# Residual-add LayerNorm on one Trainium2 core: one-pass variance, gamma and beta spread by a matmul, other chunk lists

## The chip, the cores and the metric

The kernel runs on one NeuronCore of one Trainium2 chip. The metric is device time in microseconds (us) of one execution. Most executions of one kernel here agree within about 0.3%. For one execution of each kernel there is a profile; its span (first to last instruction) is about 2 us shorter than the time.

Engines: VectorE (DVE in the profile), ScalarE (ACT), TensorE (PE), GpSimd (POOL), and SyncE (SP). SyncE and ScalarE issue DMAs on hardware queues, GpSimd on a software queue.

## The reference

```python
# x, residual: 16 x 1024 x 512 float32; gamma = ones(512), beta = zeros(512), eps = 1e-5
z = x + residual
mean = np.mean(z, axis=-1, keepdims=True)
var = np.var(z, axis=-1, keepdims=True)
return gamma * (z - mean) / np.sqrt(var + eps) + beta      # float32
```

16,384 rows of 512 numbers: 33.55 MB each for x, the residual and the output, 100.7 MB in all. There is no matmul in the task.

## The kernel before

The rows are cut into 128 blocks of 128 rows. A chunk is r blocks (r = 4 in the body, 1 or 2 at the ends). For each chunk SyncE loads x and the residual (1 MiB each for r = 4); `produce` makes the sum and the statistics; `consume`, one chunk later, scales, multiplies by gamma, adds beta, and stores from GpSimd, whose DMA casts float16 to float32.

```python
BODY_R = 4
HEAD_CHUNKS = [2, 2]
TAIL_CHUNKS = [2, 2, 1, 1, 1, 1]
BUFS = 9                      # buffers of each tile
ACT_APPLY_FRAC = 0.5          # share of a chunk's blocks that ScalarE scales

nc.gpsimd.dma_start(out=g_t[:], in_=gamma.partition_broadcast(P))   # g_t, b_t: 128 x 512 float16
nc.gpsimd.dma_start(out=b_t[:], in_=beta.partition_broadcast(P))

# produce (one chunk)
nc.sync.dma_start(out=xt[:, 0:r_cur, :], in_=x_ap)
nc.sync.dma_start(out=rt[:, 0:r_cur, :], in_=r_ap)
for n in range(r_cur):                               # VectorE: z = x + residual, S = sum of z
    nc.vector.tensor_tensor_reduce(out=xt[:, n, :], in0=xt[:, n, :], in1=rt[:, n, :],
        op0=ALU.add, op1=ALU.add, accum_out=S[:, n:n+1], ...)
nc.scalar.mul(nmean, S, -inv_D)
for n in range(r_cur):                               # ScalarE: Qc = sum of (z - mean)^2
    nc.scalar.activation(out=junk[:], in_=xt[:, n, :], func=AF.Square,
        bias=nmean[:, n:n+1], accum_out=Qc[:, n:n+1])
nc.scalar.activation(out=std, in_=Qc, func=AF.Sqrt, bias=eps_t[:], scale=inv_D)
nc.vector.reciprocal(out=rstd, in_=std)
nc.vector.tensor_mul(nmr, nmean, rstd)

# consume (the chunk before)
n_act = int(round(r_cur * ACT_APPLY_FRAC))           # 2 of 4, 1 of 2, 0 of 1
for n in range(r_cur):
    if n < n_act: nc.scalar.activation(out=ot[:, n, :], in_=xt[:, n, :], func=AF.Identity,
                      bias=nmr[:, n:n+1], scale=rstd[:, n:n+1])
    else:         nc.vector.tensor_scalar(out=ot[:, n, :], in0=xt[:, n, :], scalar1=nmean[:, n:n+1],
                      scalar2=rstd[:, n:n+1], op0=ALU.add, op1=ALU.mult)
nc.vector.tensor_mul(ot, ot, g_b)                    # float16, whole chunk
nc.vector.tensor_add(ot, ot, b_b)
nc.gpsimd.dma_start(out=o_ap, in_=ot[:, 0:r_cur, :])
# ... (cut: allocation, the loop produce(i), consume(i - 1), the launch)
```

The program is a list for each engine whose order a scheduler fixes when the kernel is built. The list is worked off in that order, so an instruction that waits holds back what is behind it (the run with the longer tail list, below, shows VectorE idle for 1.42 us in front of such an instruction).

## Time and profile before

| | before |
|---|---|
| time, median of 5 | 254.42 us (254.24 to 254.47) |
| span of the profiled run | 252.5 us |
| DMA rate in the body | 416 to 430 GB/s |
| VectorE busy / ScalarE busy | 77% / 67% of the span |
| last 4-block load pair used by VectorE from | 223.69 us |
| VectorE's last instruction ends | 247.50 us |

From the page of the kernel before: the GB/s moved in each of 40 equal slices, the chain of waits by line, and two groups of instructions (engine, operation, output <- inputs, count | busy us, mean ns of one | idle before). L107 is line 107 of the kernel as it was run; line numbers differ between the two kernels. POOLq, SPq and DVEq are the engines' queues.

```profile
GB/s 207 360 428 416 424 427 421 423 422 423 421 427 419 426 424 422 423 421 426 423 421 427 422 426 422 418 430 422 423 422 421 426 426 418 422 414 392 249 319 106
...
DMA rt<-in_residual_dram 91%; POOL out_dram L170 1%; DVE ot L157 1%; DVE ot L167 1%; DVE xt L94 1%; DVE ot L168 0%; POOLq L213 0%; SPq L85 0%; DVE nmr L126 0%; DVE rstd L123 0%; DVE S L94 0%; POOLq L170 0%; DVEq L94 0%
...
L107 ACT ACTIVATE junk<-xt,nmean 128x512 f32<-128x512 f32 x128 | 88.4, 691 | 4.0
...
L157 DVE TENSOR_SCALAR ot<-xt,nmean,rstd 128x512 f16<-128x512 f32 x66 | 33.2, 539 | 0.0
```

The reader sees a flat plateau near 423 GB/s between a weak head and a weak tail: the body is bound by DMA. "91%" means that nearly the whole chain which ends last is landing of residual loads. The square takes 691 ns for a 128x512 block.

The next line is from the view of waits (who waited for whom: us in total, times, longest): VectorE, the busiest compute engine, waited 26 times for loads, so in the body it has time to spare.

```profile
DVE xt L94 <- DMA rt<-in_residual_dram: 40.5, 26, 4.7
```

The head in 1 us windows (window, length, busy us of the engines, TensorE clock, DMA share, GB/s), and the two broadcast loads in the view of DMAs (KB, us from issue to landing):

```profile
core 0: us, DVE busy (x) ACT busy (x) POOL busy (x), PEclk, DMA share, GB/s
...
4.00:5.00 1.00, 0.00 (x0) 0.00 (x0) 0.00 (x0) 1.00 0.93 337
5.00:6.00 1.00, 0.47 (x1) 0.00 (x0) 0.00 (x0) 1.00 0.63 135
6.00:7.00 1.00, 0.85 (x4) 0.12 (x1) 0.00 (x0) 1.00 1.07 335
7.00:8.00 1.00, 0.00 (x0) 0.94 (x4) 0.00 (x0) 1.00 0.80 216
```

```profile
g_t<-in_gamma_dram POOLq DMA_DIRECT2D x1, 128.0 KB, 6.6
b_t<-in_beta_dram POOLq DMA_DIRECT2D x1, 128.0 KB, 8.7
```

DMA share is the mean busy share of the 16 DMA engines. There is a hole of 135 GB/s at 5 to 6 us, in which the DMA engines are busy for only 0.63 of the time, and less than full rate until 9 us, while the broadcasts of gamma and beta are under way (until about 8 and 11 us).

The tail on VectorE in the timeline (start, us, instruction, [idle before]):

```profile
223.69 0.69 DVE L94 CUSTOM_DVE_ANT_0 xt<-xt,rt 128x512 f32<-128x512 f32 x1 [1.50 <-DMA rt<-in_residual_dram]
...
224.98 0.16 DVE L126 TENSOR_TENSOR nmr<-nmean,rstd 128x4 f32<-128x4 f32 x1
...
226.28 1.00 DVE L157 TENSOR_SCALAR ot<-xt,nmean,rstd 128x512 f16<-128x512 f32 x2
...
227.80 1.22 DVE L167 TENSOR_TENSOR ot<-ot,g_t 128x2048 f16<-128x2048 f16 x1
...
246.05 0.54 DVE L157 TENSOR_SCALAR ot<-xt,nmean,rstd 128x512 f16<-128x512 f32 x1
246.62 0.42 DVE L167 TENSOR_TENSOR ot<-ot,g_t 128x512 f16<-128x512 f16 x1
247.08 0.42 DVE L168 TENSOR_TENSOR ot<-ot,b_t 128x512 f16<-128x512 f16 x1
```

A sum appears as two instructions, CUSTOM_DVE_ANT_0 and DVE_READ_ACCUMULATOR2_ANT. At 223.69 the last 4-block pair has landed. VectorE then makes sums (L94), between them finishes the statistics of the chunk before (nmr), scales that chunk (L157), and multiplies it by gamma (L167). It is busy nearly without gap for 23.8 us, until 247.50; 5.0 us later the span ends.

### The profile page before, as it was taken

The numbers are of one execution on the slowest core, as the hardware profiler recorded it, in microseconds if no ns is written. First come the engines' busy times: TensorE is split into PE (matmuls) and PEld (weight loads), VectorE is DVE, ScalarE is ACT, GpSimd is POOL, SyncE is SP. The second block draws the span as 40 slices with busy tenths as digits, with TensorE's granted clock in tenths as the row PEclk, the third lists the DMA queues.
The fourth block names the chain that finished last, engine by engine and source line by source line (L and its number), as shares of the span: only waits on it lengthen the run. The fifth ranks groups of instructions, "written<-read, shape, count | busy, mean of one in ns | idle before, by whom it ended". The sixth has DMA issues, their size and how long they took to land.

```text
span 252.5 us, 1223 instructions
## 1 busy us (share of the span) xinstructions
DVE 195.7 (77%) x471; ACT 168.2 (67%) x394; POOL 21.3 (8%) x43
## 2 busy tenths in 40 slices
DVE  1255899999678877788788886789877888779992
ACT  2374888888456785676786664787665688569760
POOL 2000000000000000000000000000000000000221
DMA  6999999999999999999999999999999999999693
GB/s 207 360 428 416 424 427 421 423 422 423 421 427 419 426 424 422 423 421 426 423 421 427 422 426 422 418 430 422 423 422 421 426 426 418 422 414 392 249 319 106
DMA packets 16282, 101.01 MB, mean 400 GB/s; under 512 B 1808, under 2 KB 2064, under 8 KB 5136
## 3 DMA queue, kind: packets, MB, share of 16 engines
q1 hardware_dynamic: 10656, 67.11, 69.4%
q0 software_dynamic: 5616, 33.82, 34.5%
q14 instruction: 10, 0.08, 0.1%
HBM read 67.63 MB, written 33.55 MB: 401 GB/s over the span
## 4 chain that ended last, share of the span: by engine, by line
DMA 91%; issue 3%; DVE 3%; POOL 1%; POOLq 0%; SPq 0%; DVEq 0%
DMA rt<-in_residual_dram 91%; POOL out_dram L170 1%; DVE ot L157 1%; DVE ot L167 1%; DVE xt L94 1%; DVE ot L168 0%; POOLq L213 0%; SPq L85 0%; DVE nmr L126 0%; DVE rstd L123 0%; DVE S L94 0%; POOLq L170 0%; DVEq L94 0%
## 5 line engine op out<-in xcount | busy, mean ns | idle before, releaser
L94 DVE CUSTOM_DVE_ANT_0 xt<-xt,rt 128x512 f32<-128x512 f32 x128 | 84.6, 680 | 40.5 <-DMA rt<-in_residual_dram 40.5
L107 ACT ACTIVATE junk<-xt,nmean 128x512 f32<-128x512 f32 x128 | 88.4, 691 | 4.0
L149 ACT ACTIVATE ot<-xt,nmr,rstd 128x512 f16<-128x512 f32 x62 | 47.3, 806 | 56.4 <-DVE nmr L126 56.4
L167 DVE TENSOR_TENSOR ot<-ot,g_t 128x2048 f16<-128x2048 f16 (+2 forms) x37 | 39.9, 1078 | 3.9 <-ACT ot L149 1.0
L168 DVE TENSOR_TENSOR ot<-ot,b_t 128x2048 f16<-128x2048 f16 (+2 forms) x37 | 39.9, 1078 | 1.1
L170 POOL DMA_DIRECT2D out_dram<-ot x37 | 19.9, 539 | 225.9 <-ACT junk L107 197.8
L157 DVE TENSOR_SCALAR ot<-xt,nmean,rstd 128x512 f16<-128x512 f32 x66 | 33.2, 539 | 0.0
L107 ACT ACTIVATION_READ_ACCUMULATOR junk<-xt,nmean 128x1 f32 x128 | 23.8, 186 | 0.0
L105 ACT ACTIVATE nmean<-S 128x4 f32<-128x4 f32 (+2 forms) x37 | 7.1, 191 | 15.0 <-DVE S L94 15.0
L115 ACT ACTIVATE std<-Qc,eps_t 128x4 f32<-128x4 f32 (+2 forms) x37 | 11.0, 296 | 1.1
L123 DVE RECIPROCAL rstd<-std 128x4 f32<-128x4 f32 (+2 forms) x37 | 6.3, 169 | 5.5 <-ACT std L115 5.3
L94 DVE DVE_READ_ACCUMULATOR2_ANT S<- 128x1 f32 x128 | 10.4, 81 | 0.0
L126 DVE TENSOR_TENSOR nmr<-nmean,rstd 128x4 f32<-128x4 f32 (+2 forms) x37 | 5.8, 156 | 0.1
L105 ACT ACT_TABLE_LOAD x1 | 1.3, 1283 | 0.7 <-PEq L199 0.7
L115 ACT ACT_TABLE_LOAD x1 | 1.3, 1283 | 0.0
L68 POOL DMA_DIRECT2D g_t<-in_gamma_dram x1 | 0.7, 669 | 0.8 <-PEq L213 0.8
L71 DVE MEMSET eps_t<- 128x1 f32 x1 | 0.1, 59 | 0.8 <-PEq L199 0.8
L69 POOL DMA_DIRECT2D b_t<-in_beta_dram x1 | 0.5, 540 | 0.0
L199 POOL MEMSET const-float32-0.0<- 128x1 f32 x1 | 0.1, 98 | 0.2 <-issue 0.2
L199 POOL MEMSET const-bfloat16-1.0<- 128x1 bf16 x1 | 0.1, 101 | 0.0
L199 POOL MEMSET const-uint8-127<- 128x1 uint8 x1 | 0.1, 99 | 0.0
L199 POOL MEMSET const-float32-1.0<- 128x1 f32 x1 | 0.1, 98 | 0.0
## 6 DMA issues: line engine op xcount, KB each, us to landing
xt<-in_x_dram SPq DMA_DIRECT2D x29, 1024.0 KB, 29.6
rt<-in_residual_dram SPq DMA_DIRECT2D x29, 1024.0 KB, 29.7
out_dram<-ot POOLq DMA_DIRECT2D x29, 1024.0 KB, 9.4
xt<-in_x_dram SPq DMA_DIRECT2D x4, 512.0 KB, 16.6
rt<-in_residual_dram SPq DMA_DIRECT2D x4, 512.0 KB, 16.2
out_dram<-ot POOLq DMA_DIRECT2D x4, 512.0 KB, 6.3
xt<-in_x_dram SPq DMA_DIRECT2D x4, 256.0 KB, 11.9
rt<-in_residual_dram SPq DMA_DIRECT2D x4, 256.0 KB, 9.6
```

Of the source, the lines that this page charges most:

```text
L68: nc.gpsimd.dma_start(out=g_t[:], in_=gamma.partition_broadcast(P))
L94: nc.vector.tensor_tensor_reduce(out=xt[:, n, :], in0=xt[:, n, :], in1=rt[:, n, :], scale=1.0, scalar=0.0, op0=ALU.add, op1=ALU.add, accum ...
L105: nc.scalar.mul(nmean[:, 0:r_cur], S[:, 0:r_cur], -inv_D)
L107: nc.scalar.activation(out=junk[:], in_=xt[:, n, :], func=AF.Square, bias=nmean[:, n : n + 1], accum_out=Qc[:, n : n + 1],)
L115: nc.scalar.activation(out=std[:, 0:r_cur], in_=Qc[:, 0:r_cur], func=AF.Sqrt, bias=eps_t[:], scale=inv_D,)
L123: nc.vector.reciprocal(out=rstd[:, 0:r_cur], in_=std[:, 0:r_cur])
L126: nc.vector.tensor_mul(nmr[:, 0:r_cur], nmean[:, 0:r_cur], rstd[:, 0:r_cur])
L149: nc.scalar.activation(out=ot[:, n, :], in_=xt[:, n, :], func=AF.Identity, bias=nmr[:, n : n + 1], scale=rstd[:, n : n + 1],)
L157: nc.vector.tensor_scalar(out=ot[:, n, :], in0=xt[:, n, :], scalar1=nmean[:, n : n + 1], scalar2=rstd[:, n : n + 1], op0=ALU.add, op1=ALU. ...
L167: nc.vector.tensor_mul(ot[:, 0:r_cur, :], ot[:, 0:r_cur, :], g_b)
L168: nc.vector.tensor_add(ot[:, 0:r_cur, :], ot[:, 0:r_cur, :], b_b)
L170: nc.gpsimd.dma_start(out=o_ap, in_=ot[:, 0:r_cur, :])
```

## The change

Four independent things, besides renaming and reformatting: (1) gamma and beta come as two rows of 2 KB from ScalarE's queue, and a matmul with a column of ones spreads each over 128 partitions; (2) the small head chunks go; (3) the tail list has five chunks instead of six; (4) the variance is taken as E[z^2] - mean^2, so that the square needs no mean and can start after the first block's sum.

```diff
-HEAD_CHUNKS = [2, 2]
-TAIL_CHUNKS = [2, 2, 1, 1, 1, 1]
+HEAD_CHUNKS: list[int] = []
+TAIL_CHUNKS: list[int] = [2, 2, 2, 1, 1]
+CENTERED_STATS = False
+PIPE_DEPTH = 1
-    nc.gpsimd.dma_start(out=g_t[:], in_=gamma.partition_broadcast(P))
-    nc.gpsimd.dma_start(out=b_t[:], in_=beta.partition_broadcast(P))
+    ones = consts.tile([1, P], FP32, name="ones")
+    nc.vector.memset(ones[:], 1.0)
+    nc.scalar.dma_start(out=g_row[:], in_=gamma.unsqueeze(0))
+    nc.scalar.dma_start(out=b_row[:], in_=beta.unsqueeze(0))
+    for row, dst in ((g_row, g_t), (b_row, b_t)):
+        ps = psum.tile([P, D], FP32, ...)
+        nc.tensor.matmul(ps[:], lhsT=ones[:], rhs=row[:], start=True, stop=True)
+        nc.vector.tensor_copy(dst[:], ps[:])
...
         for n in range(r_cur):
             nc.vector.tensor_tensor_reduce(... accum_out=S[:, n : n + 1])
+            nc.scalar.activation(out=junk[:], in_=xt[:, n, :], func=AF.Square,
+                                 accum_out=Qc[:, n : n + 1])
         nc.scalar.mul(nmean, S, -inv_D)
-        for n in range(r_cur):
-            nc.scalar.activation(out=junk[:], in_=xt[:, n, :], func=AF.Square,
-                                 bias=nmean[:, n : n + 1], accum_out=Qc[:, n : n + 1])
-        nc.scalar.activation(out=std, in_=Qc, func=AF.Sqrt, bias=eps_t[:], scale=inv_D)
+        nc.scalar.activation(out=msq, in_=S, func=AF.Square, scale=inv_D)
+        nc.vector.scalar_tensor_tensor(out=var, in0=Qc, scalar=inv_D, in1=msq,
+                                       op0=ALU.mult, op1=ALU.subtract)
+        nc.scalar.activation(out=std, in_=var, func=AF.Sqrt, bias=eps_t[:])
```

The changed file keeps the old statistics behind its flag. With the flag and the other three parts set back, its instruction lists equal those of the kernel before on every engine, so nothing else in the diff matters.

More of the change, by code (lines that the diff above doesn't have):

```diff
@@ L19 @@
 ACT_APPLY_FRAC = 0.5
-DUAL_QUEUE_LOADS = False
+CENTERED_STATS = False
+PIPE_DEPTH = 1
 @with_exitstack
@@ L45 @@
     n_blocks = N // P
-    chunks: list[int] = []
     head = [c for c in HEAD_CHUNKS if c <= BODY_R]
@@ L67 @@
     b_t = consts.tile([P, D], o_dt, name="b_t")
-    nc.gpsimd.dma_start(out=g_t[:], in_=gamma.partition_broadcast(P))
-    nc.gpsimd.dma_start(out=b_t[:], in_=beta.partition_broadcast(P))
+    ones = consts.tile([1, P], FP32, name="ones")
+    nc.vector.memset(ones[:], 1.0)
+    g_row = consts.tile([1, D], FP32, name="g_row")
+    b_row = consts.tile([1, D], FP32, name="b_row")
+    nc.scalar.dma_start(out=g_row[:], in_=gamma.unsqueeze(0))
+    nc.scalar.dma_start(out=b_row[:], in_=beta.unsqueeze(0))
+    for row, dst in ((g_row, g_t), (b_row, b_t)):
+        ps = psum.tile([P, D], FP32, name="ps_" + ("g" if dst is g_t else "b"))
+        nc.tensor.matmul(ps[:], lhsT=ones[:], rhs=row[:], start=True, stop=True)
+        nc.vector.tensor_copy(dst[:], ps[:])
     eps_t = consts.tile([P, 1], FP32, name="eps_t")
@@ L74, with produce @@
     state: list[dict | None] = []
-    def produce(st, base_block, r_cur):
+    def produce(base_block, r_cur):
         rows = P * r_cur
@@ L85, in produce @@
         nc.sync.dma_start(out=xt[:, 0:r_cur, :], in_=x_ap)
-        (nc.scalar if DUAL_QUEUE_LOADS else nc.sync).dma_start(
-            out=rt[:, 0:r_cur, :], in_=r_ap
-        )
+        nc.sync.dma_start(out=rt[:, 0:r_cur, :], in_=r_ap)
         S = stats.tile([P, BODY_R], FP32, name="S")
         Qc = stats.tile([P, BODY_R], FP32, name="Qc")
-        for n in range(r_cur):
-            nc.vector.tensor_tensor_reduce(
-                out=xt[:, n, :],
-                in0=xt[:, n, :],
-                in1=rt[:, n, :],
-                scale=1.0,
-                scalar=0.0,
-                op0=ALU.add,
-                op1=ALU.add,
-                accum_out=S[:, n : n + 1],
-            )
@@ L104, in produce @@
-        nmean = stats.tile([P, BODY_R], FP32, name="nmean")
-        nc.scalar.mul(nmean[:, 0:r_cur], S[:, 0:r_cur], -inv_D)
-        for n in range(r_cur):
-            nc.scalar.activation(
-                out=junk[:],
-                in_=xt[:, n, :],
-                func=AF.Square,
-                bias=nmean[:, n : n + 1],
-                accum_out=Qc[:, n : n + 1],
-            )
-        std = stats.tile([P, BODY_R], FP32, name="std")
-        nc.scalar.activation(
-            out=std[:, 0:r_cur],
-            in_=Qc[:, 0:r_cur],
-            func=AF.Sqrt,
-            bias=eps_t[:],
-            scale=inv_D,
-        )
@@ L122, in produce @@
-        rstd = stats.tile([P, BODY_R], FP32, name="rstd")
+        nmean = stats.tile([P, BODY_R], FP32, name="nmean")
+        std = stats.tile([P, BODY_R], FP32, name="std")
+        rstd = stats.tile([P, BODY_R], FP32, name="rstd")
+        nmr = stats.tile([P, BODY_R], FP32, name="nmr")
+        if CENTERED_STATS:
+            for n in range(r_cur):
+                nc.vector.tensor_tensor_reduce(
+                    out=xt[:, n, :], in0=xt[:, n, :], in1=rt[:, n, :],
+                    scale=1.0, scalar=0.0, op0=ALU.add, op1=ALU.add,
+                    accum_out=S[:, n : n + 1],
+                )
+            nc.scalar.mul(nmean[:, 0:r_cur], S[:, 0:r_cur], -inv_D)
+            for n in range(r_cur):
+                nc.scalar.activation(
+                    out=junk[:], in_=xt[:, n, :], func=AF.Square,
+                    bias=nmean[:, n : n + 1], accum_out=Qc[:, n : n + 1],
+                )
+            nc.scalar.activation(
+                out=std[:, 0:r_cur], in_=Qc[:, 0:r_cur], func=AF.Sqrt,
+                bias=eps_t[:], scale=inv_D,
+            )
+        else:
+            for n in range(r_cur):
+                nc.vector.tensor_tensor_reduce(
+                    out=xt[:, n, :], in0=xt[:, n, :], in1=rt[:, n, :],
+                    scale=1.0, scalar=0.0, op0=ALU.add, op1=ALU.add,
+                    accum_out=S[:, n : n + 1],
+                )
+                nc.scalar.activation(
+                    out=junk[:], in_=xt[:, n, :], func=AF.Square,
+                    accum_out=Qc[:, n : n + 1],
+                )
+            nc.scalar.mul(nmean[:, 0:r_cur], S[:, 0:r_cur], -inv_D)
+            msq = stats.tile([P, BODY_R], FP32, name="msq")
+            nc.scalar.activation(
+                out=msq[:, 0:r_cur], in_=S[:, 0:r_cur], func=AF.Square, scale=inv_D
+            )
+            var = stats.tile([P, BODY_R], FP32, name="var")
+            nc.vector.scalar_tensor_tensor(
+                out=var[:, 0:r_cur], in0=Qc[:, 0:r_cur], scalar=inv_D,
+                in1=msq[:, 0:r_cur], op0=ALU.mult, op1=ALU.subtract,
+            )
+            nc.scalar.activation(
+                out=std[:, 0:r_cur], in_=var[:, 0:r_cur], func=AF.Sqrt,
+                bias=eps_t[:],
+            )
@@ L123, in produce @@
         nc.vector.reciprocal(out=rstd[:, 0:r_cur], in_=std[:, 0:r_cur])
-        nmr = stats.tile([P, BODY_R], FP32, name="nmr")
         if ACT_APPLY_FRAC > 0:
-            nc.vector.tensor_mul(
-                nmr[:, 0:r_cur], nmean[:, 0:r_cur], rstd[:, 0:r_cur]
-            )
+            nc.vector.tensor_mul(nmr[:, 0:r_cur], nmean[:, 0:r_cur], rstd[:, 0:r_cur])
         return dict(
-            base_block=base_block,
-            r_cur=r_cur,
-            xt=xt,
-            ot=ot,
-            nmean=nmean,
-            rstd=rstd,
-            nmr=nmr,
+            base_block=base_block, r_cur=r_cur,
@@ L137, in produce @@
+            xt=xt, ot=ot, nmean=nmean, rstd=rstd, nmr=nmr,
         )
@@ L149, in consume @@
                 nc.scalar.activation(
-                    out=ot[:, n, :],
-                    in_=xt[:, n, :],
-                    func=AF.Identity,
-                    bias=nmr[:, n : n + 1],
-                    scale=rstd[:, n : n + 1],
+                    out=ot[:, n, :], in_=xt[:, n, :], func=AF.Identity,
+                    bias=nmr[:, n : n + 1], scale=rstd[:, n : n + 1],
                 )
@@ L157, in consume @@
                 nc.vector.tensor_scalar(
-                    out=ot[:, n, :],
-                    in0=xt[:, n, :],
-                    scalar1=nmean[:, n : n + 1],
-                    scalar2=rstd[:, n : n + 1],
-                    op0=ALU.add,
-                    op1=ALU.mult,
+                    out=ot[:, n, :], in0=xt[:, n, :],
+                    scalar1=nmean[:, n : n + 1], scalar2=rstd[:, n : n + 1],
+                    op0=ALU.add, op1=ALU.mult,
                 )
@@ L175 @@
     for i, r_cur in enumerate(chunks):
-        state.append(produce(i, base_block, r_cur))
-        state[i]["base_block"] = base_block
+        state.append(produce(base_block, r_cur))
         base_block += r_cur
-        if i >= 1:
-            consume(state[i - 1])
-            state[i - 1] = None
-    consume(state[-1])
+        j = i - PIPE_DEPTH
+        if j >= 0 and state[j] is not None:
+            consume(state[j])
+            state[j] = None
+    for c in state:
+        if c is not None:
+            consume(c)
 _INS = ['x', 'residual', 'gamma', 'beta', 'eps']
```

## The prediction

> **What bounds the kernel now.** The DMA engines, for about 220 of 252.5 us. The page's slices show 416 to 428 GB/s from slice 3 to slice 35, and the chain of waits gives 91% to the landing of residual loads. The Trainium skill ("DMA: Bandwidth & Descriptors", Bandwidth) puts the fabric ceiling at 435 GB/s and 16 MB transfers at 425; the trace's 423 agrees. The bytes (67.1 MB in, 33.6 MB out) cannot shrink, so the floor is about 100.7/0.423 = 238 us; the other 14 us are head and tail.
>
> - Head (1 us windows): 2 to 9 us moves about 1.98 MB where 423 GB/s would give 2.96, with a hole of 135 GB/s at 5 to 6 us. The two broadcast loads of gamma and beta (issued 1.3 and 1.9 us, 6.6 and 8.7 us to landing) lie exactly there.
> - Tail (timeline): the last 4-block load pair lands at 223.6 us; from there VectorE is busy nearly without gap until 247.5. DMA falls to 38 GB/s at 236 to 238 us: loads are over and stores wait for VectorE. Then 5 us for last store and end.
>
> In between VectorE waits 40.5 us in 26 waits for loads, about 1.5 us of each 7.4 us chunk; ACT has more slack.
>
> **What the change does.**
> 1. Statistics by E[z²]−mean²: Square no longer waits for nmean; per chunk it adds one ACT Square of 128x4 (about 0.2 us, like nmean's 0.19) and one VectorE subtraction (about 0.16, like nmr's 0.157), and the round trip ACT, VectorE, ACT, VectorE. The built instruction order shows that VectorE now does a chunk's statistics and its scaling before it takes the next load: 4 x 0.61 + 2 x 1.22 + 0.16 + 0.30 + 0.17 + 0.16 + 1.0 = about 6.8 us per chunk, against 6.24 before (spacing of stores while catching up at 32 to 57 us). That is still below the DMA's 7.4 us, so the body doesn't move: VectorE's waits shrink from about 1.5 to 0.6 us per chunk.
> 2. Gamma and beta as two 2 KB rows spread by matmul: 0.25 MB less written and no broadcast packets. Loads should run near 420 GB/s soon after 3 us. Up to 2.9 us could be won (0.98 + 0.25 MB at 423); I take 1.8, as part of the hole may be ordinary start-up. The two PSUM copies delay VectorE by about 1 us, but nothing in the DMA.
> 3. No small head chunks: first compute starts near 8 us instead of 5.5, hidden behind loads.
> 4. Tail [2,2,2,1,1] instead of [2,2,1,1,1,1]: VectorE saves about 0.8 us (gamma and beta 5.7 instead of 6.0, one fewer scaling), the new subtraction costs 0.7 of it; the chunk before is already scaled when the last big load lands (1.0 less), some stalls on ACT round trips come back. Net −0.6 us.
>
> **Prediction:** 252.0 us (−1.8 head, −0.6 tail), range 250.0 to 254.4. Faster by over 2%: 0.05; within 2%: 0.92; slower: 0.03.
>
> **What would show it.** Head: no 135 GB/s hole between 5 and 9 us; last big residual load landing near 222. Body: unchanged 423 GB/s, store spacing about 7.4 us, VectorE's wait for residual loads below 25 us in total. Tail: VectorE ends about 22.5 to 23.5 us after the last big landing.
>
> **What would make it wrong.** The head hole is not the broadcasts' doing (gain 0.5); the statistics round trip lengthens VectorE's chunk beyond 7.4 us, so that it becomes the limit of the body (+10 us or more); the fixed tail order makes VectorE wait for a landing with work left behind it (+2).

## The result, and the profile after

The changed kernel took 250.43 us (median of 8, 250.33 to 250.55) against 254.46 us (median of 15): ratio 0.984, 95% interval 0.9831 to 0.985. A ratio is the mean time of one kernel's fast runs over that of the other's in the same rounds, so not quite the ratio of the medians quoted. The time is inside the predicted range and within 2%, but the gain is 4.0 us where 2.4 was predicted. Output was correct, here and in all runs below.

From the page of the changed kernel, the same lines as before:

```profile
GB/s 265 422 426 421 397 421 421 424 422 422 422 422 425 421 422 426 422 422 424 424 422 425 422 421 424 424 425 424 424 424 421 422 422 424 422 418 410 343 273 169
...
DMA rt<-in_residual_dram 90%; DMA xt<-in_x_dram 2%; DVE xt L122 1%; DVE ot L176 1%; DVE ot L175 1%; POOL out_dram L178 0%; DVE ot L168 0%; ACT ot L163 0%; POOLq L223 0%; DVE var L137 0%; ACT junk L127 0%; DVE rstd L145 0%; DVE nmr L147 0%; DVE S L122 0%; ACT nmean L131 0%
...
L127 ACT ACTIVATE junk<-xt 128x512 f32<-128x512 f32 x128 | 76.3, 596 | 30.6 <-ACT ot L163 15.4
...
L168 DVE TENSOR_SCALAR ot<-xt,nmean,rstd 128x512 f16<-128x512 f32 x65 | 33.1, 545 | 0.0
```

The plateau is at the same height; head and tail are fuller (265 and 422 GB/s in the first two slices instead of 207 and 360). The square is 95 ns shorter. This agrees with the Trainium skill, "ScalarE: Activation LUTs", What ACT_TABLE_LOAD costs: each per-partition pointer operand adds about 93 ns, and the square has lost its bias (691 to 596 ns). From the view of waits: VectorE's reserve in the body is halved, but not used up.

```profile
DVE xt L122 <- DMA rt<-in_residual_dram: 19.2, 22, 1.5
```

The head in windows (this page has columns for TensorE too): no hole.

```profile
core 0: us, PE busy (x) PEld busy (x) DVE busy (x) ACT busy (x) POOL busy (x), PEclk, DMA share, GB/s
...
4.00:5.00 1.00, 1.00 (x2) 0.00 (x0) 0.00 (x0) 0.00 (x0) 0.00 (x0) 1.00 0.96 393
5.00:6.00 1.00, 0.44 (x2) 0.10 (x1) 0.61 (x1) 0.25 (x1) 0.00 (x0) 1.00 0.93 379
6.00:7.00 1.00, 1.00 (x2) 0.40 (x2) 0.07 (x1) 1.00 (x1) 0.00 (x0) 1.00 1.11 467
7.00:8.00 1.00, 0.97 (x2) 0.00 (x0) 0.00 (x0) 0.03 (x1) 0.00 (x0) 1.00 1.01 426
```

The tail on VectorE:

```profile
219.45 0.16 DVE L147 TENSOR_TENSOR nmr<-nmean,rstd 128x4 f32<-128x4 f32 x1
219.53 1.00 DVE L168 TENSOR_SCALAR ot<-xt,nmean,rstd 128x512 f16<-128x512 f32 x2
221.25 0.69 DVE L122 CUSTOM_DVE_ANT_0 xt<-xt,rt 128x512 f32<-128x512 f32 x1 [0.71 <-DMA rt<-in_residual_dram]
...
223.70 0.08 DVE L122 DVE_READ_ACCUMULATOR2_ANT S<- 128x1 f32 x1
223.70 1.22 DVE L175 TENSOR_TENSOR ot<-ot,g_t 128x2048 f16<-128x2048 f16 x1
...
225.45 0.08 DVE L122 DVE_READ_ACCUMULATOR2_ANT S<- 128x1 f32 x1
225.45 0.15 DVE L137 SCALAR_TENSOR_TENSOR var<-Qc,msq 128x4 f32<-128x4 f32 x1
225.53 1.21 DVE L176 TENSOR_TENSOR ot<-ot,b_t 128x2048 f16<-128x2048 f16 x1
...
241.79 0.54 DVE L168 TENSOR_SCALAR ot<-xt,nmean,rstd 128x512 f16<-128x512 f32 x1
242.24 0.41 DVE L176 TENSOR_TENSOR ot<-ot,b_t 128x512 f16<-128x512 f16 x1
242.58 0.42 DVE L175 TENSOR_TENSOR ot<-ot,g_t 128x512 f16<-128x512 f16 x1
243.03 0.42 DVE L176 TENSOR_TENSOR ot<-ot,b_t 128x512 f16<-128x512 f16 x1
```

The last 4-block pair is taken up at 221.25, 2.44 us earlier than before. The chunk before it was already scaled (219.53), so gamma and beta (L175, L176) follow directly on the four sums. VectorE ends at 243.45, 22.2 us after the landing, where it had needed 23.8. With 4.85 us instead of 5.0 from there to the end of the span, the 4.2 us between the spans split into 2.4 (head) + 1.6 (tail) + 0.15.

### The profile page after: what moved, and what is told of

Same layout as the page of the kernel before. It is cut to its first block, busy times and chain, and to the rows that moved or that the text cites. A ratio compares the mean times of both kernels' runs of the same rounds, so it can differ in the third digit from the quotient of the medians.

```text
span 248.3 us, 1338 instructions
## 1 busy us (share of the span) xinstructions
PE 4.1 (2%) x4; PEld 1.0 (0%) x4; DVE 201.3 (81%) x500; ACT 155.9 (63%) x426; POOL 19.3 (8%) x39
## 4 chain that ended last, share of the span: by engine, by line
DMA 92%; DVE 3%; issue 2%; ACT 0%; POOL 0%; POOLq 0%; DVEq 0%
DMA rt<-in_residual_dram 90%; DMA xt<-in_x_dram 2%; DVE xt L122 1%; DVE ot L176 1%; DVE ot L175 1%; POOL out_dram L178 0%; DVE ot L168 0%; ACT ot L163 0%; POOLq L223 0%; DVE var L137 0%; ACT junk L127 0%; DVE rstd L145 0%; DVE nmr L147 0%; DVE S L122 0%; ACT nmean L131 0%
## 5 line engine op out<-in xcount | busy, mean ns | idle before, releaser
L122 DVE CUSTOM_DVE_ANT_0 xt<-xt,rt 128x512 f32<-128x512 f32 x128 | 81.2, 685 | 19.2 <-DMA rt<-in_residual_dram 19.2
L127 ACT ACTIVATE junk<-xt 128x512 f32<-128x512 f32 x128 | 76.3, 596 | 30.6 <-ACT ot L163 15.4
L163 ACT ACTIVATE ot<-xt,nmr,rstd 128x512 f16<-128x512 f32 x63 | 47.9, 805 | 13.5 <-DVE nmr L147 13.5
L176 DVE TENSOR_TENSOR ot<-ot,b_t 128x2048 f16<-128x2048 f16 (+2 forms) x35 | 39.6, 1132 | 1.0
L175 DVE TENSOR_TENSOR ot<-ot,g_t 128x2048 f16<-128x2048 f16 (+2 forms) x35 | 39.4, 1127 | 0.1
L178 POOL DMA_DIRECT2D out_dram<-ot x35 | 19.1, 545 | 224.8 <-ACT std L141 185.3
L141 ACT ACTIVATE std<-var,eps_t 128x4 f32<-128x4 f32 (+2 forms) x35 | 10.3, 295 | 34.0 <-DVE var L137 34.0
L127 ACT ACTIVATION_READ_ACCUMULATOR junk<-xt 128x1 f32 x128 | 23.9, 187 | 0.0
L137 DVE SCALAR_TENSOR_TENSOR var<-Qc,msq 128x4 f32<-128x4 f32 (+2 forms) x35 | 5.4, 154 | 2.5 <-ACT junk L127 2.5
L133 ACT ACTIVATE msq<-S 128x4 f32<-128x4 f32 (+2 forms) x35 | 6.6, 189 | 0.0
L77 DVE CAST g_t<-ps_g 128x512 f16<-128x512 f32 x1 | 0.7, 690 | 4.4 <-PE ps_g L76 4.4
L76 PE MATMUL ps_g<-g_row,ones 1*128 1x512 f32 x2 | 2.0, 1122 | 3.3 <-DMA g_row<-in_gamma_dram 3.3
L76 PE MATMUL ps_b<-b_row,ones 1*128 1x512 f32 x2 | 2.1, 1136 | 0.6 <-DMA b_row<-in_beta_dram 0.6
```

The costliest lines, as they stand in the source:

```text
L133: nc.scalar.activation(out=msq[:, 0:r_cur], in_=S[:, 0:r_cur], func=AF.Square, scale=inv_D)
L141: nc.scalar.activation(out=std[:, 0:r_cur], in_=var[:, 0:r_cur], func=AF.Sqrt, bias=eps_t[:],)
L175: nc.vector.tensor_mul(ot[:, 0:r_cur, :], ot[:, 0:r_cur, :], g_b)
L176: nc.vector.tensor_add(ot[:, 0:r_cur, :], ot[:, 0:r_cur, :], b_b)
```

## The experiments

Four calls, all with five rounds beside the kernel before on the same chip (its median was 254.34 to 254.40 in each). First each part alone, put into the kernel before.

**Only the constants**

```diff
-    nc.gpsimd.dma_start(out=g_t[:], in_=gamma.partition_broadcast(P))     # and beta
+    nc.scalar.dma_start(out=g_row[:], in_=gamma.unsqueeze(0))             # and beta; then matmul, copy
```

> The kernel before, with only gamma and beta brought in as two 2 KB rows and spread by matmul. Theory A (the two broadcast loads make the slow head): the hole of 135 GB/s at 5 to 6 us goes, the last 4-block load pair lands near 221.5 us instead of 223.6, time -1.8 to -2.5 us. Theory B (the small head chunks make the slow head): at most -0.7 us, the hole stays.

252.15 us, ratio 0.9911 (0.9897 to 0.9924): 2.2 us won. The last pair is taken up at 221.74 instead of 223.69; VectorE's tail is 23.81 us, exactly as before. Theory A held: of the head's two candidates, the broadcasts make the slow stretch.

**Only the head list**

```diff
-HEAD_CHUNKS = [2, 2]
+HEAD_CHUNKS = []
```

> The kernel before, with only the two 2-block head chunks replaced by the ordinary 4-block chunks. Theory A: 0 to -0.5 us, hole at 5 to 6 us still there. Theory B: -1.8 us or more, and the hole goes.

254.23 us, ratio 0.9993 (0.9979 to 1.0006): no gain beyond noise. The slow stretch stays, moved to 6 to 9 us (285, 251 and 274 GB/s). Theory B fell.

**Only the tail list**

```diff
-TAIL_CHUNKS = [2, 2, 1, 1, 1, 1]
+TAIL_CHUNKS = [2, 2, 2, 1, 1]
```

> The kernel before, with only the tail list [2,2,2,1,1] in place of [2,2,1,1,1,1]. Theory C (most of the 1.6 us won in the tail comes from the order that the new statistics give to VectorE): -0.3 to -0.7 us here. Theory D (it comes from fewer and larger tail chunks): -1.2 us or more here.

253.88 us, ratio 0.998 (0.9968 to 0.9993): 0.5 us. The tail on VectorE is 23.05 us.

**Only the statistics**

```diff
-bias=nmean[:, n : n + 1] in the Square; std from Qc
+no bias; var = Qc/D - (S/D)^2; std from var
```

> The kernel before, with only the statistics taken as E[z^2]-mean^2. Theory C: -0.8 to -1.5 us, all of it after the last 4-block pair has landed, because VectorE has scaled the chunk before already and ends sooner after that landing. Theory D: within 0.4 us of before. Body at 423 GB/s in both.

253.80 us, ratio 0.9978 (0.9966 to 0.9991): 0.5 us. The tail is 23.40 us. Neither C nor D: each theory wanted one of the two to carry the tail's gain, and neither does. The four parts sum to 3.3 us, the change gives 4.0. So something works only together.

**The change without the tail list, and without the statistics**

```diff
-TAIL_CHUNKS: list[int] = [2, 2, 2, 1, 1]        # first kernel
+TAIL_CHUNKS: list[int] = [2, 2, 1, 1, 1, 1]
-CENTERED_STATS = False                          # second kernel
+CENTERED_STATS = True
```

> The changed kernel with the old tail list [2,2,1,1,1,1]. The four parts done alone gave -2.2, -0.1, -0.5 and -0.5 us, together -3.3, while the change gives -4.0: 0.7 us come only from parts together. If the parts were simply additive this run loses 0.5 us against the changed kernel (ratio to before 0.986). If the missing 0.7 us is tail list and statistics together, it loses about 1.2 us (0.9885).

> The changed kernel with the old, centered statistics. Additive: loses 0.5 us (ratio 0.986). Tail list and statistics together: loses about 1.2 us (0.9885). If the statistics work with the constants instead (VectorE starts late in both), only this run and not the one with the old tail loses over 1 us.

251.72 us, ratio 0.9895 (0.9879 to 0.991), and 251.77 us, ratio 0.9896 (0.9883 to 0.991). Each loses 1.3 us against the changed kernel, 0.5 if they were additive. So the two parts together are worth about 1.6 us on top of constants and head list (an estimate: 254.3 - 2.2 - 0.1 = 252.0 without them, 250.4 with them), and each alone some 0.3 to 0.5. Both runs lose over 1 us, so the third possibility, statistics with the constants alone, falls.

**The change without the head list**

```diff
-HEAD_CHUNKS: list[int] = []
+HEAD_CHUNKS: list[int] = [2, 2]
```

> The changed kernel with the two small head chunks back. If the head list works only through the interaction, it loses 0.8 us (ratio 0.987); if it is worth nothing, it stays within 0.2 us of the changed kernel (0.984 to 0.985).

250.78 us, ratio 0.9859 (0.9846 to 0.9873): about 0.4 us lost, between the two expectations, and its single runs spread more than others (250.49 to 251.20). The head list is worth little. Its VectorE tail is that of the change (22.17 us).

The profiled runs say where the tail's 1.6 us are. The table adds up VectorE's time from the last 4-block landing to its end, each instruction counted from its start to the start of the next one (with the count of instructions; idle time is set apart):

| | before | only tail list | only statistics | the change |
|---|---|---|---|---|
| sums, 12 | 7.28 | 7.44 | 7.38 | 7.33 |
| scalings | 4.78 (10) | 4.26 (9) | 4.04 (8) | 3.35 (7) |
| times gamma, plus beta | 9.96 (16) | 9.65 (14) | 9.90 (16) | 9.72 (14) |
| rstd, nmr | 1.42 (16) | 1.37 (14) | 1.04 (14) | 1.01 (12) |
| var | - | - | 0.59 (7) | 0.45 (6) |
| waits for a landing, others | 0.37 | 0.33 | 0.45 | 0.34 |
| sum, us | 23.81 | 23.05 | 23.40 | 22.20 |

The tail list takes away one scaling (a 1-block chunk is scaled on VectorE alone, a 2-block chunk half) and one chunk's small instructions. The statistics change the order: two scalings and the small instructions of one chunk are done before the landing, in time in which VectorE had waited. Both have instructions leave VectorE's tail, which has hardly a gap. In the profiled runs the four parts taken singly shorten the span by 3.1 us and the change by 4.2. Of the 1.1 us between, 0.68 are in VectorE's tail (0.44 between the columns above; 0.24 because the head list alone had it at 24.05 us), 0.26 in the landing, and 0.18 between last store and end. Why the scheduler's order for both parts has fewer exposed latencies was not isolated. The end of the timeline shows one: in the kernel before the last block's scaling, gamma and beta stand alone (246.05 to 247.50), in the changed one they are interleaved with those of the block before (241.79 to 243.45).

**What is slow about the broadcasts?** Two kernels, both with only the constants touched: the first edit is against the kernel before, the second against "only the constants".

```diff
-    nc.gpsimd.dma_start(out=g_t[:], in_=gamma.partition_broadcast(P))     # and beta
+    nc.scalar.dma_start(out=g32[:], in_=gamma.partition_broadcast(P))     # float32, hardware queue; and beta
+    nc.vector.tensor_copy(g_t[:], g32[:])
```

> The kernel before, with gamma and beta broadcast to 128 partitions by two DMAs from ScalarE's hardware queue in float32 (0.52 MB written instead of 0.26) and cast by VectorE. Theory A1 (broadcast packets as such are slow): no gain, or a loss up to 1 us, and low GB/s between 3 and 9 us. Theory A2 (the software queue or its cast makes them slow): about 1.0 to 1.5 us faster than before, with over 380 GB/s in 3 to 9 us.

```diff
+    # gamma and beta by matmul, and two DMAs that nothing reads, from rows of their own:
+    nc.gpsimd.dma_start(out=dummy[:, 0, :], in_=x_f[64 * P : 65 * P, :])
+    nc.gpsimd.dma_start(out=dummy[:, 1, :], in_=x_f[65 * P : 66 * P, :])
```

> The kernel before with gamma and beta spread by matmul, plus two DMAs that nothing uses, issued where the two broadcasts were: same software queue, same cast from float32 to float16, same 128 packets of 2 KB each, but each packet from a row of its own in x instead of 128 times the same row. The run without them took 252.15 us, the kernel before 254.3. If reading one row 128 times is what is slow (theory A1), these cost only their bytes, 0.26 MB at 423 GB/s = 0.6 us: about 252.8 us, and over 370 GB/s in 2 to 9 us. If the queue, the cast or the 2 KB packets are slow (theory A3), they cost the 2 us again: about 254.3 us, and under 330 GB/s of traffic there.

The broadcast on the hardware queue took 254.41 us, ratio 1.0001 (0.9988 to 1.0013); the dummy rows 253.54 us, ratio 0.9964 (0.995 to 0.9977). Traffic from 2 to 9 us in the view of windows, one fence each for: the kernel before; only the constants; broadcast on the hardware queue; dummy rows.

```profile
2.00:9.00 7.00, 1.31 (x4) 1.85 (x6) 0.46 (x1) 1.00 0.88 283
```

```profile
2.00:9.00 7.00, 3.75 (x4) 1.11 (x4) 2.93 (x7) 1.59 (x3) 0.00 (x0) 1.00 1.00 387
```

```profile
2.00:9.00 7.00, 0.62 (x2) 0.94 (x1) 0.00 (x0) 1.00 0.82 308
```

```profile
2.00:9.00 7.00, 4.11 (x4) 1.00 (x4) 2.69 (x6) 1.59 (x3) 0.47 (x1) 1.00 1.03 344
```

The last number is GB/s, the one before it the DMA share. Taking off the constants' own bytes (0.26, 0, 0.52 and 0.26 MB), x and residual moved 1.72, 2.71, 1.63 and 2.15 MB in these 7 us. At 423 GB/s, what is missing against the second is 2.3, 2.6 and 1.3 us; the times differ by 2.2, 2.3 and 1.4 us. (The single runs of the dummy rows fall into two groups, 253.24 to 253.29 and 253.79 to 253.96, so their cost is 1.4 give or take 0.3.) So the software queue is not needed for the loss: the hardware queue shows it too, though it is no exact repeat, since it writes twice the bytes and casts nothing.

The DMA share separates two costs. With the dummy rows the engines are never idle (1.03). Their 256 packets, which read 2 KB and write 1 KB each, fill 12.4% of the 16 engines' time from 0 to 13 us (`prof dummy_rows --dma --window 0:13`), that is 1.6 us, where 0.26 MB at 423 GB/s would be an estimated 0.6. This is enough for their whole cost of 1.4 us. The packets of the broadcasts take no longer: 12.4% again on the software queue and 10.8% (1.4 us) on the hardware queue. But there the engines also stand idle, for 12% and 18% of the 7 us (0.8 and 1.3 us; 0.65 of the 1.3 from 2 to 3 us, where the run with only the head list, whose broadcast packets had not begun, is idle for 0.54 too). So A3 fits the larger part, the time that so many small packets take, and A1 the rest: of these four runs only the two whose packets all read one row left the engines idle on average. Why the engines idle then was not isolated, and a software and a hardware queue with the same bytes were not compared.

**Is the tail really VectorE's?** More of the scaling to ScalarE:

```diff
-ACT_APPLY_FRAC = 0.5
+ACT_APPLY_FRAC = 0.75
```

> The changed kernel with ScalarE's share of the scaling raised from 0.5 to 0.75: in the tail 7 scalings of 0.53 us leave VectorE (one is left), ScalarE gets 6 more of 0.8 us. If VectorE's busy time sets the length of the tail, as the split of the runs so far says, VectorE ends about 19.5 us after the last 4-block load pair instead of 22.2, and the time falls by about 2 us to 248.4. If the chain of round trips or the loads set it, the time stays within 0.4 us of 250.4 or grows. The body stays at 423 GB/s either way.

252.35 us, ratio 0.9916 (0.9903 to 0.9929): 1.9 us *slower* than the change. VectorE's busy time in the tail fell as expected, from 21.8 to 19.75 us, but 4.5 us of idle time came up. From VectorE's timeline, four of the multiplications that waited; then, from ScalarE's (`prof act75 --timeline --engine ACT --window 236:246`), its last two scalings:

```profile
238.27 0.69 DVE L175 TENSOR_TENSOR ot<-ot,g_t 128x1024 f16<-128x1024 f16 x1 [0.33 <-ACT ot L163]
...
240.48 0.69 DVE L175 TENSOR_TENSOR ot<-ot,g_t 128x1024 f16<-128x1024 f16 x1 [0.71 <-ACT ot L163]
...
242.85 0.42 DVE L175 TENSOR_TENSOR ot<-ot,g_t 128x512 f16<-128x512 f16 x1 [0.81 <-ACT ot L163]
...
244.68 0.42 DVE L175 TENSOR_TENSOR ot<-ot,g_t 128x512 f16<-128x512 f16 x1 [0.88 <-ACT ot L163]
```

```profile
242.00 0.81 ACT L163 ACTIVATE ot<-xt,nmr,rstd 128x512 f16<-128x512 f32 x1 [0.57 <-DVE nmr L147]
...
243.84 0.81 ACT L163 ACTIVATE ot<-xt,nmr,rstd 128x512 f16<-128x512 f32 x1 [0.84 <-DVE nmr L147]
```

Five of the seven multiplications by gamma in the tail now wait for ScalarE's scaling (L163), 0.3 to 0.9 us a time. At the last two 2-block chunks ScalarE came late, busy without a gap from 235.74 us until then. At the two 1-block chunks it had itself waited 0.57 and 0.84 us for VectorE's nmr: a round trip between the engines, with nothing else in front of VectorE. In this tail VectorE is busy for 19.8 us and ScalarE for 19.2 (in the change 21.8 and 14.3). So VectorE's busy time was the length of the tail only as long as ScalarE kept ahead; the expectation's first branch, made from one engine's busy time, was wrong, and its second, that the round trips set the time, fits. (Six scalings left VectorE, not the seven that its text says.)

**A shorter lag into the tail**

```diff
-TAIL_CHUNKS: list[int] = [2, 2, 2, 1, 1]
+TAIL_CHUNKS: list[int] = [2, 2, 2, 2, 2, 1, 1]     # first kernel
+TAIL_CHUNKS: list[int] = [3, 3, 2, 2, 1, 1]        # second kernel
```

> The changed kernel with tail list [2,2,2,2,2,1,1] instead of [2,2,2,1,1]: the last 12 blocks instead of 8 come in small chunks, so that VectorE is one 2-block chunk behind the loads, not one 4-block chunk, when the last loads arrive. If the lag that VectorE brings into the tail sets its length, 2 blocks less to finish are about 1.5 us: near 249.0 us. Against it: one fixed cost per chunk more (0.3 to 0.5 us of VectorE), 4 KB packets for 2 MB more of loads, and more round trips between ScalarE and VectorE; if these win, 250.4 or more.

> The changed kernel with tail list [3,3,2,2,1,1]: chunks shrink step by step, and rounding gives ScalarE 2 of 3 scalings in the 3-block chunks, which is a small step of the move that failed with 6 scalings. If a lag of 3 blocks instead of 4 and about one scaling less on VectorE count, near 249.5 us; if round trips with ScalarE count more, 250.4 or more.

The first took 252.11 us, ratio 0.9907 (0.9892 to 0.9921), 1.7 us slower than the change; the second 250.44 us, ratio 0.9839 (0.9823 to 0.9856), the same as the change. VectorE's timeline of the first:

```profile
231.32 0.09 DVE L122 DVE_READ_ACCUMULATOR2_ANT S<- 128x1 f32 x1
231.32 0.55 DVE L168 TENSOR_SCALAR ot<-xt,nmean,rstd 128x512 f16<-128x512 f32 x1
233.29 0.69 DVE L122 CUSTOM_DVE_ANT_0 xt<-xt,rt 128x512 f32<-128x512 f32 x1 [1.42 <-DMA rt<-in_residual_dram]
...
237.67 0.16 DVE L145 RECIPROCAL rstd<-std 128x2 f32<-128x2 f32 x1
239.07 0.69 DVE L122 CUSTOM_DVE_ANT_0 xt<-xt,rt 128x512 f32<-128x512 f32 x1 [1.24 <-DMA rt<-in_residual_dram]
```

VectorE has caught up with the loads, and its fixed order puts two sums in front of other work: it idles 1.4 and 1.2 us for landings. The order is not the whole cause: the last load's packets end at 238.6 us, in the change at 235.9, though it was issued sooner (223.83 against 224.61 us); stores ran beside it. Had it landed as in the change, the second wait could not have lasted until 239.07. Why it landed late was not isolated. A smaller lag was reached and did not pay. No version here beats the change.

## Why the prediction was right

The time (250.43) was in the range (250.0 to 254.4) and in the predicted class. The mechanisms held; two terms of the sum were too small, both in the same direction, so the time came out near the lower end of a range that reached up to no gain at all.

- **The body doesn't move: right.** 423 GB/s in both. VectorE's wait for loads fell to 19.2 us (predicted: below 25). Its chunk, read from the spacing of stores while it catches up (28.50 to 35.09 us), is 6.6 us, predicted 6.8; a DMA-bound chunk takes 7.4.
- **The head, "I take 1.8": direction right, size 2.2 by the time of the constants alone.** The hole was nearly all the broadcasts' doing. The discount for "ordinary start-up" was too large: it took 1.1 us off the 2.9, while without the broadcasts 387 GB/s instead of 423 from 2 to 9 us leave 0.6 (352 to 446 GB/s from 3 us on). The landing moved to 221.2, predicted "near 222".
- **No small head chunks, "hidden behind loads": right**, within 0.4 us.
- **The tail, "Net -0.6 us": direction right, size 1.6.** VectorE ended 22.2 us after the landing, outside the predicted 22.5 to 23.5. The scalings were sized well (three fewer: 1.4 us, predicted 0.5 + 1.0). Predicted for the new subtraction: 0.7 us; measured 0.45: after each of the six the next instruction starts some 0.075 us later, though each is listed at 0.154. The Trainium skill, "Perfetto Trace Analysis", Optimizing Scalar/DVE Operations, says that an instruction's fixed data-access overhead shows in the profile at about twice its busy time, since the write half overlaps with the next instruction; this trace agrees (0.154 against 0.075 for instructions of 4 elements a partition or fewer), and the prediction had taken one at "about 0.16", its listed duration. Left out altogether: four fewer rstd and nmr (0.4 us). And some half a microsecond set aside for "stalls on ACT round trips" did not appear: the waits are 0.34 us, before 0.37.
- **That tail list and statistics are worth more together** was not foreseen: the prediction added their terms. Each alone is worth 0.5 us, the pair 1.6.
- The third risk it names, a fixed order that makes VectorE wait for a landing, did not occur in the change, but did with the longer list of small chunks.

The plateau behind the prediction's floor of 238 us agrees with the Trainium skill, "DMA: Bandwidth & Descriptors", Bandwidth (425 GB/s for one load of 16 MB): 423 here, for loads and stores together.

Open: why the landing shifts by 0.7 to 0.8 us between profiled runs whose bytes are the same (221.99 without the statistics, 222.08 without the head list, 221.25 with all); why the time from last store to end varies from 4.5 to 5.2 us.

## What to carry to other kernels

In a kernel bound by DMA in its body, look for the gain at the ends: here what the loads missed in the head came back almost one to one (2.3 us missing, 2.2 us of time, from 0.26 MB of broadcast). Before a small row is broadcast over 128 partitions by DMA beside the first loads, try to bring it once and spread it on an idle engine, which won those 2.2 us here. In the tail add up the busiest engine's work by start-to-start spacing from the last landing on, but check before moving work that the other engine stays ahead: an engine full without gaps is only a bound for as long as nothing makes it wait.

## What the Trainium skill lacked or had wrong

- "DMA: Bandwidth & Descriptors" has nothing on what it costs when all packets of a load read one row. Here 128 packets reading 2 KB of one row, twice, cost 2.2 us beside other loads, from the software and the hardware queue alike (254.4 us both), with the DMA engines idle for 12% and 18% of 2 to 9 us; packets of the same size from rows of their own cost 1.4 us, with no idle engines.
- The same page says in Bandwidth, "Where 436 GB/s comes from", that for transfers between HBM and SBUF the HBM side (about 358 GB/s) binds. With one core running, 423 GB/s held for 200 us. "HBM Reference", Specifications (TRN2), has this right (about 425 for a core alone).
